# Weights and matmul operands moved to other byte positions in SBUF by padding

## The chip, the core and the metric

One core of a Trainium2 chip runs the program. The metric is the device time of one execution in microseconds. The kernel before took 2636.11 us as the median of three runs (2630.96 to 2636.66).

## What is computed

A stack of transformer blocks on 256 tokens of width 1024 in fp32. Two layers work on two streams, `x` and `ctx`: a gated feed-forward (1024 to 2816 and back), a token mixer (neighbourhood attention with a pooled branch, and attention to the context), and a second feed-forward; each is normed, modulated and added back. Then the stream `x` alone goes through a dilated attention mixer, a feed-forward, a chunkwise mLSTM mixer, and a last feed-forward and norm. Nearly all of the arithmetic is `h @ w` with a weight matrix that is read once:

```python
def swiglu(h, w_gate_up, w_down):
    gate, up = jnp.split(h @ w_gate_up, 2, axis=-1)
    return (jax.nn.silu(gate) * up) @ w_down
```

## The kernel before, in words

Activations lie transposed: 128 of the 1024 channels on the partitions, 8 such rows `k`, and the 256 tokens along the free dimension. A product keeps fp32 accuracy with three matmuls in the format fp32r: weight and operand are each split into a high and a low part, and `wh*xh`, `wh*xl` and `wl*xh` are added up in one PSUM bank. So each 128x128 block of a weight is loaded three times (`whi`, `whi`, `wlo`), and each load is followed by one matmul that streams 256 columns, or 258 where two columns carry the shift of the modulation.

The weights come as pieces of 1024 columns (4096 bytes in each partition). `Weights.fetch` (lines 80 to 85) has SP load a piece into one of three buffers `raw`; `Weights.cut` (lines 87 to 98) has ScalarE round it into `whi` and VectorE subtract that into `wlo`, each in a ring of six buffers. `wk` (lines 129 and 130) takes block k, 512 bytes wide, out of a piece. The pool `raw` and the pool `w` are opened in `build` (lines 1508 and 1509), right behind the constants.

The normed stream is `hh` and `hl`, one pair for each of the streams a and b (lines 1529 to 1533): 8 rows of `NP` = 272 floats, of which 258 are used. `gemm` (lines 270 to 280) streams row k of `hh`, `hl`, `hh` against block k of each of its weights, k from 0 to 7: this is the gate and up product (tile `gu`), the mixers' projections (`qkv`, `qk`, `ps_v`, `ps_o`). The way back is `blocks` (lines 587 to 602, matmuls on lines 598 to 600): it streams the rows of `s.ah` and `s.al`, 1024 bytes each, into `ps_dn` (feed-forward) or `ps_wo` (mixers). Where those tiles are allocated is in `ffn_two` (tiles `aha`, `ala`, `ahb`, `alb`), `ffn_one` (`ah`, `al`, one stream), `token_mix` (`oha`, `ola`, `ohb`, `olb`), `dilated_mix` and `mlstm_mix` (`oh`, `ol`). The order of the instructions on TensorE is the program's own (`manual_schedule`): a matmul waits only for its operands and its bank.

In a partition the tiles of the pools lie one behind the other in the order in which they are opened, each rounded up to 32 bytes. Counted in bytes of a partition, the tiles that TensorE reads start at:

| tile | before, start modulo 1024 | step from row to row |
|---|---|---|
| `whi`, `wlo`, every buffer | 96 | 512 (a block) |
| `hha`, `hla` | 480, 992 | 1088 |
| `hhb`, `hlb` | 512, 0 | 1088 |
| `aha`, `ala`, `ahb`, `alb`, `oha`, `ola`, `ohb`, `olb` | 544 | 1024 |
| `ah`, `al`; `oh`, `ol` of both single-stream mixers | 512 | 1024 |
| `pth`, `ptl` of the dilated mixer (streamed) | 768 | 1024 |
| `vh`, `vl` of the dilated mixer (loaded), groups 0 and 1 | 768 | 512 |

Of the kernel before, what the change touches and what calls it, by code (L numbers as in the profile page):

```python
# [9 lines left out]
F32 = mybir.dt.float32  # L10
F32R = mybir.dt.float32r
# [7 lines left out]
P = 128  # L19
T = 256  # L20
NS = 258
NP = 272
D = 1024
KD = D // P
FF = 2816
# [107 lines left out]
class Kernel:  # L133
# [9 lines left out]
    def plan(self):  # L143
# [27 lines left out]
        def mix(l):  # L171
# [5 lines left out]
            wout(("wo", l), A["w_out"][l])  # L177

        ffn_two(0, 0)
        mix(0)  # L180
        ffn_two(0, 1)
        ffn_two(1, 0)
        mix(1)
        ffn_one(("f", 1, 1), A["w_gu"][1, 1], A["w_down1"])
        for b in range(36):
            pair(("att",), A["attn_w_in"][b])
        wout(("awo",), A["attn_w_out"])
        ffn_one(("s", 0), A["ffn_w_in"][0], A["ffn_w_out"][0])
        p.append((("mg",), A["mlstm_gates"]))
        for b in range(12):  # L190
            pair(("ml",), A["mlstm_w_in"][b])
        wout(("mwo",), A["mlstm_w_out"])
        ffn_one(("s", 1), A["ffn_w_in"][1], A["ffn_w_out"][1])
        return p

# [431 lines left out]
    def ffn_two(self, l, i, first, nxts, start):  # L627

        nc = self.nc
        key = ("f", l, i)  # L630
        n = 0 if i == 0 else 2
        mods = self.mods[l, i]
        sa, sb = self.pair
        with ExitStack() as es:
            self.fp = pool = es.enter_context(self.tc.tile_pool(name="ffn", bufs=1))
            for s in self.pair:
                s.ah = pool.tile([P, HF, T], F32R, name="ah" + s.name)
                s.al = pool.tile([P, HF, T], F32R, name="al" + s.name)
                s.y = pool.tile([P, KD, T], F32, name="y" + s.name)

            def evac(s, ps, jj):
                self.defer(s.ch, lambda: self.gu_evac(s, ps, jj, NS))

            for h in range(2):
                for jj in range(HF):
                    j = h * HF + jj
                    if j < len(first):
                        w, ps = first[j]
                        evac(sa, ps, jj)
                        evac(sb, self.gu_mm(sb, w, NS, together=j == 0), jj)  # L650
                    else:
                        if j == len(first):
                            self.drain(sa.ch)
                            self.load_cond(pool)
                            self.mod_plan = deque(m for n in mods for m in mods[n])
                        w = self.gu_weights(key, j)
                        for s in self.pair:
                            evac(s, self.gu_mm(s, w, NS), jj)
                            self.drain(s.ch)
                    self.mod_chunks(mods.get(j, ()))  # L660
                w = Chunks(lambda: self.W.get(key + ("dn",)))
                for s, ds in self.lagged(self.pair, LAG if h else 0):
                    if s is sa:
                        for d in ds:
                            self.mod_chunks(mods.get(KF + h * KD + d, ()))
                    for d, ps in self.blocks(s, ds, lambda d, c: w(HF * d + c), HF, "ps_dn"):
                        y = s.y[:, d, :]
                        if h == 0:
                            nc.scalar.activation(out=y, in_=ps, func=AF.Copy)
                            continue  # L670
                        with self.tc.high_priority(offset=FIRST):
                            nc.vector.tensor_tensor(out=y, in0=ps, in1=y, op=ALU.add)
                            if d == 0:
                                s.acc = self.new_acc(s)
                            self.square_into(s.acc, y, d == 0)
                        if d == KD - 1:
                            self.post(s, self.g5(s, l, n), s.y, nxts[s.i], WAIT[s.i])
            return self.handover(start, sa, sb)
# [13 lines left out]
    def ffn_one(self, key, s, n, first, post, nxt, start):  # L692

        nc = self.nc
        with ExitStack() as es:
            self.fp = pool = es.enter_context(self.tc.tile_pool(name="ffn", bufs=1))
            s.ah = pool.tile([P, KF, T], F32R, name="ah")
            s.al = pool.tile([P, KF, T], F32R, name="al")
            y = pool.tile([P, KD, T], F32, name="y") if post else None
            for j in range(KF):  # L700
                if j < len(first):
                    ps = first[j][1]
                else:
                    if j == len(first):
                        self.drain(s.ch)
                    ps = self.gu_mm(s, self.gu_weights(key, j), n)
                self.defer(s.ch, lambda ps=ps, j=j: self.gu_evac(s, ps, j, n))
            acc = None
            w = Chunks(lambda: self.W.get(key + ("dn",)))
            for ds in ((0, 1), *((d,) for d in range(2, KD))):  # L710
                for d, ps in self.blocks(s, ds, lambda d, c: w(KF * d + c), KF, "ps_dn"):
                    if post:
                        self.keep(s, d, ps, y[:, d, :])
                    else:
                        acc = self.residual(s, d, ps, nxt, acc)
            if post:
                self.post(s, post, y, (nxt, None), WAIT[2])
            return self.handover(start, s)
# [508 lines left out]
    def mlstm_mix(self, s, first, nxt, start):  # L1227
        with ExitStack() as es:
            op = es.enter_context(self.tc.tile_pool(name="mlo", bufs=1))
            s.ah = op.tile([P, KD, T], F32R, name="oh")  # L1230
            s.al = op.tile([P, KD, T], F32R, name="ol")
            self.mp = es.enter_context(self.tc.tile_pool(name="ml", bufs=2))
            att, vch = self.mlstm_core(s, first)
            self.wout_one(("mwo",), s, nxt, att, 2)
            self.end(vch, att)
            return self.handover(start, s)
# [251 lines left out]
    def build(self):  # L1488
        tc, nc, A = self.tc, self.nc, self.A
# [14 lines left out]
        with ExitStack() as es:  # L1504
            ec = es.enter_context
            ec(tc.manual_schedule(engines={mybir.EngineType.PE}))
            self.const = const = ec(tc.tile_pool(name="const", bufs=1))
            rawp = ec(tc.tile_pool(name="raw", bufs=RAW))
            wp = ec(tc.tile_pool(name="w", bufs=RING))
            self.tmp = ec(tc.tile_pool(name="tmp", bufs=2))  # L1510
            self.psp = ec(tc.tile_pool(name="psp", bufs=8, space=PSUM))
            self.wch = self.chain()
            self.W = Weights(tc, rawp, wp, self.plan(), RING - 1, 3)
# [5 lines left out]
            self.ident = self.cst("ident")  # L1519
            self.modv = [const.tile([P, NMODC, 2], F32, name="modv%d" % l) for l in range(2)]  # L1520

            sa, sb = self.pair = [Stream(), Stream()]
            hp_a = ec(tc.tile_pool(name="sa", bufs=1))
            es_b = ExitStack()
            hp_b = es_b.enter_context(tc.tile_pool(name="sb", bufs=1))
            for i, (s, hp) in enumerate(((sa, hp_a), (sb, hp_b))):
                s.i, s.name = i, "ab"[i]
                s.ch = self.chain()
                s.x = hp.tile([P, KD, T], F32, name="x" + s.name)
                s.hh = hp.tile([P, KD, NP], F32R, name="hh" + s.name)  # L1530
                s.hl = hp.tile([P, KD, NP], F32R, name="hl" + s.name)
                s.r = hp.tile([P, NS], F32, name="r" + s.name)
                nc.vector.memset(s.r[:, T:NS], 1.0)

            nx = lambda l, n: [(self.gs1(s, l, n), (l, n)) for s in self.pair]
            fin = lambda name, o=0: (lambda c: self.par(name, o + c, 1))
# [187 lines left out]
```

## Time and profile before

| | |
|---|---|
| median of three runs | 2636.11 us |
| the profiled execution | 2636.68 us |
| its span, first to last instruction | 2634.9 us |
| mean granted TensorE clock | 0.97 of full speed |
| TensorE matmuls | 20335, busy 2527.3 us |
| weight loads | 20335, busy 2451.9 us |
| VectorE, ScalarE, GpSimd busy | 1857.8, 1171.5, 75.2 us |

Matmuls overlap in the profile (one is shown as some 0.28 us long), so what a matmul costs is read as the distance from one start to the next in the timeline, not from its length.

### The profile page before, as it was taken

To read this page: it belongs to the slowest core of one execution; us is meant where nothing else is said; L and a number is where in the kernel's file an instruction comes from. 1 tells how busy PE (TensorE), PEld (TensorE's weight loads), DVE (VectorE), ACT (ScalarE), POOL (GpSimd) and SP (SyncE) were. 2 spreads that over 40 slices of the span, in tenths; PEclk is the share of its full clock that TensorE was granted. 3 is DMA by queue.
4 is the path that set the end of the run, shared out by engine and by line. 5 is a ranking of instruction groups with operands and counts; after the bars stand their busy time and mean duration, and the time that the engine had idled before them with its cause. 6 is when DMAs were issued, how large, how long until landed. Compare 5 with 4: busy or idle time off the path is not lost. (4 is left out here: it accounts for less than half of the span.)

```text
span 2634.9 us, 49868 instructions
## 1 busy us (share of the span) xinstructions
PE 2527.3 (96%) x20335; PEld 2451.9 (93%) x20335; DVE 1857.8 (71%) x3734; ACT 1171.5 (44%) x2062; POOL 75.2 (3%) x131
## 2 busy tenths in 40 slices
PE   7999998999999999999999888998999999999998
PEld 5999997889999999999998778998999999978998
DVE  5998548676998546984547767757888676666764
ACT  4332324664432333332334555545655554565542
POOL 0000001210000000000000310000000000000000
PEclk9999998999999999999999988999999999988999
DMA  8666323622566321674222734554444365533653
GB/s 300 205 212 207 105 89 74 79 45 73 184 204 222 103 96 58 225 254 153 97 93 77 87 69 149 195 184 136 149 149 149 131 205 181 173 104 103 202 176 120
DMA packets 105254, 383.17 MB, mean 145 GB/s; under 512 B 13560, under 2 KB 13688, under 8 KB 103360
## 3 DMA queue, kind: packets, MB, share of 16 engines
q1 hardware_dynamic: 101984, 370.89, 42.2%
q0 software_dynamic: 3040, 9.09, 4.3%
q8 instruction: 159, 2.61, 0.4%
q14 instruction: 71, 0.58, 0.1%
HBM read 378.88 MB, written 1.05 MB: 144 GB/s over the span
## 5 line engine op out<-in xcount | busy, mean ns | idle before, releaser
L94 ACT ACTIVATE whi<-raw 128x1024 fp32r<-128x1024 f32 x559 | 588.3, 1054 | 566.3 <-PE gu L278 172.4
L96 DVE TENSOR_TENSOR wlo<-raw,whi 128x1024 fp32r<-128x1024 f32 x559 | 680.8, 1220 | 222.8 <-ACT whi L94 220.3
L279 PE MATMUL gu<-hha,wlo 128*128 128x258 f32 (+1 forms) x2112 | 602.4, 285 | 9.0 <-DVE wlo L96 9.0
L277 PE MATMUL gu<-hha,whi 128*128 128x258 f32 (+1 forms) x2112 | 601.8, 285 | 4.3 <-ACT hha L254 2.5
L278 PE MATMUL gu<-hla,whi 128*128 128x258 f32 (+1 forms) x2112 | 602.5, 285 | 1.0 <-DVE hla L255 1.0
L279 PEld LDWEIGHTS gu<-hha,wlo 128*128 128x128 f32 x2112 | 406.5, 192 | 10.8 <-DVE wlo L96 10.8
L277 PEld LDWEIGHTS gu<-hha,whi 128*128 128x128 f32 x2112 | 406.5, 192 | 5.4 <-ACT hha L254 3.1
L278 PEld LDWEIGHTS gu<-hla,whi 128*128 128x128 f32 x2112 | 405.4, 192 | 2.0 <-DVE hla L255 1.9
L278 PE MATMUL gu<-hlb,whi 128*128 128x258 f32 x1056 | 301.1, 285 | 1.3 <-DVE hlb L255 1.0
L277 PE MATMUL gu<-hhb,whi 128*128 128x258 f32 x1056 | 299.8, 284 | 1.1 <-ACT hhb L254 1.1
L279 PE MATMUL gu<-hhb,wlo 128*128 128x258 f32 x1056 | 295.9, 280 | 0.0
L278 PEld LDWEIGHTS gu<-hlb,whi 128*128 128x128 f32 x1056 | 200.6, 190 | 2.3 <-DVE hlb L255 2.3
L277 PEld LDWEIGHTS gu<-hhb,whi 128*128 128x128 f32 x1056 | 200.6, 190 | 1.5 <-ACT hhb L254 1.5
L279 PEld LDWEIGHTS gu<-hhb,wlo 128*128 128x128 f32 x1056 | 202.0, 191 | 0.0
L503 DVE SCALAR_TENSOR_TENSOR junk<-wm,cond 128x1024 bf16<-128x1024 f32 x128 | 156.3, 1221 | 41.9 <-DMA wm<-w_mod 41.0
L599 PE MATMUL ps_dn<-ala,whi 128*128 128x256 f32 x528 | 146.2, 277 | 2.2 <-DVE ala L252 2.2
L599 PE MATMUL ps_dn<-al,whi 128*128 128x256 f32 x528 | 148.2, 281 | 0.0
L598 PE MATMUL ps_dn<-ah,whi 128*128 128x256 f32 x528 | 148.2, 281 | 0.0
L600 PE MATMUL ps_dn<-ah,wlo 128*128 128x256 f32 x528 | 148.2, 281 | 0.0
L598 PE MATMUL ps_dn<-ahb,whi 128*128 128x256 f32 x528 | 147.7, 280 | 0.0
L599 PE MATMUL ps_dn<-alb,whi 128*128 128x256 f32 x528 | 147.1, 279 | 0.0
L600 PE MATMUL ps_dn<-ahb,wlo 128*128 128x256 f32 x528 | 147.1, 279 | 0.0
(413 smaller groups left out, 6024.4 us busy)
## 6 DMA issues: line engine op xcount, KB each, us to landing
raw<-w_gu SPq DMA_DIRECT2D x176, 512.0 KB, 3.8
wm<-w_mod SPq DMA_DIRECT2D x128, 512.0 KB, 4.2
raw<-w_down SPq DMA_DIRECT2D x88, 512.0 KB, 3.4
raw<-ffn_w_in SPq DMA_DIRECT2D x88, 512.0 KB, 3.6
raw<-attn_w_in SPq DMA_DIRECT2D x72, 512.0 KB, 3.4
raw<-ffn_w_out SPq DMA_DIRECT2D x44, 512.0 KB, 3.3
raw<-w_in SPq DMA_DIRECT2D x32, 512.0 KB, 3.3
raw<-mlstm_w_in SPq DMA_DIRECT2D x24, 512.0 KB, 3.5
```

The costliest lines, as they stand in the source:

```text
L94: nc.scalar.activation(out=hi[:, :n], in_=raw[:, :n], func=AF.Copy)
L96: nc.vector.tensor_tensor(out=lo[:, :n], in0=raw[:, :n], in1=hi[:, :n].bitcast(F32), op=ALU.subtract)
L277: nc.tensor.matmul(o, wh, xh, start=k == 0, stop=False)
L278: nc.tensor.matmul(o, wh, xl, start=False, stop=False)
L279: nc.tensor.matmul(o, wl, xh, start=False, stop=k == KD - 1)
L503: nc.vector.scalar_tensor_tensor(out=out, in0=w, scalar=1.0, in1=self.cond[:, i, :], op0=ALU.mult, op1=ALU.mult, accum_out=m[:, i:i + 1],)
L598: nc.tensor.matmul(o, wh, xh, start=i == 0, stop=False)
L599: nc.tensor.matmul(o, wh, xl, start=False, stop=False)
L600: nc.tensor.matmul(o, wl, xh, start=False, stop=i == n - 1)
```

## The change

It adds padding and reorders the allocation, and nothing else: no instruction is added or removed. The row of the streams `hh`, `hl` becomes 288 floats (1152 bytes) in stream a and 320 floats (1280 bytes) in stream b. The two tiles `r` move from the stream's pool into the pool of constants, followed by 864 bytes of padding; the pool `tmp` gets 640 bytes; `ffn_two` gets 512 bytes ahead of stream b's tiles, `ffn_one` 256 bytes ahead of `ah`, and `mlstm_mix` 64 bytes ahead of `oh`.

```diff
-NP = 272
+NP = 288, 320
...
             for s in self.pair:
+                if s is sb:
+                    pool.tile([P, 128], F32, name="padb")
                 s.ah = pool.tile([P, HF, T], F32R, name="ah" + s.name)
...
+            pool.tile([P, 64], F32, name="pado")
             s.ah = pool.tile([P, KF, T], F32R, name="ah")
...
+            op.tile([P, 16], F32, name="padm")
             s.ah = op.tile([P, KD, T], F32R, name="oh")
...
             self.const = const = ec(tc.tile_pool(name="const", bufs=1))
+            sa, sb = self.pair = [Stream(), Stream()]
+            for s, n in zip(self.pair, "ab"):
+                s.r = const.tile([P, NS], F32, name="r" + n)
+            const.tile([P, 216], F32, name="pad")
...
             self.tmp = ec(tc.tile_pool(name="tmp", bufs=2))
+            self.tmp.tile([P, 160], F32, name="padt", bufs=1)
...
                 s.ch = self.chain()
+                nc.vector.memset(s.r[:, T:NS], 1.0)
                 s.x = hp.tile([P, KD, T], F32, name="x" + s.name)
-                s.hh = hp.tile([P, KD, NP], F32R, name="hh" + s.name)
-                s.hl = hp.tile([P, KD, NP], F32R, name="hl" + s.name)
-                s.r = hp.tile([P, NS], F32, name="r" + s.name)
-                nc.vector.memset(s.r[:, T:NS], 1.0)
+                s.hh = hp.tile([P, KD, NP[i]], F32R, name="hh" + s.name)
+                s.hl = hp.tile([P, KD, NP[i]], F32R, name="hl" + s.name)
```

Added up in the same way, the starts modulo 1024 become: `whi`, `wlo` 0; `hha`, `hla` 0 with rows 1152 bytes apart; `hhb`, `hlb` 0 with rows 1280 bytes apart; `aha`, `ala` 0; `ahb`, `alb` 512; `oha`, `ola`, `ohb`, `olb` 0; `ah`, `al` 256; `oh`, `ol` 0 in the dilated mixer and 64 in the mLSTM mixer.

## Rows read from the trace of the kernel before

**Rows 1.** The page, part 1 (busy us, share, count) and granted clock in 40 slices.
```profile
PE 2527.3 (96%) x20335; PEld 2451.9 (93%) x20335; DVE 1857.8 (71%) x3734; ACT 1171.5 (44%) x2062; POOL 75.2 (3%) x131
...
PEclk9999998999999999999999988999999999988999
```
**Rows 2.** Waits of TensorE, longest in total (us, times, longest).
```profile
PE ps_bc L315 <- DVE rt L292: 23.4, 10, 6.1
```
**Rows 3.** TensorE by line and shape (xcount, busy us, mean ns).
```profile
L277 PE MATMUL gu<-hha,whi 128*128 128x258 f32 x1408 | 403.8, 287 | 4.3 <-ACT hha L254 2.5 <-ACT whi L94 1.1 <-DVE hhb L340 0.8
...
L277 PE MATMUL gu<-hhb,whi 128*128 128x258 f32 x1056 | 299.8, 284 | 1.1 <-ACT hhb L254 1.1
...
L599 PE MATMUL ps_dn<-al,whi 128*128 128x256 f32 x528 | 148.2, 281 | 0.0
...
L599 PE MATMUL ps_dn<-ala,whi 128*128 128x256 f32 x528 | 146.2, 277 | 2.2 <-DVE ala L252 2.2
...
L277 PE MATMUL qkv<-hhb,whi 128*128 128x258 f32 x192 | 64.2, 335 | 3.2 <-ACT hhb L254 2.9
...
L598 PE MATMUL ps_wo<-oh,whi 128*128 128x256 f32 x128 | 37.6, 294 | 0.0
...
L598 PE MATMUL ps_wo<-oha,whi 128*128 128x256 f32 x128 | 35.8, 279 | 0.0
...
L598 PE MATMUL ps_wo<-ohb,whi 128*128 128x256 f32 x64 | 18.0, 281 | 0.0
```
**Rows 4.** Timeline, two-stream down product: first and last of 20 matmuls (start, length us).
```profile
999.79 0.28 PE L599 MATMUL ps_dn<-ala,whi 128*128 128x256 f32 x1
...
1001.94 0.28 PE L600 MATMUL ps_dn<-aha,wlo 128*128 128x256 f32 x1
```
**Rows 5.** Timeline of the weight loads in the same stretch: one load.
```profile
999.90 0.19 PEld L598 LDWEIGHTS ps_dn<-aha,whi 128*128 128x128 f32 x1
```
**Rows 6.** Timeline, a later two-stream down product: first and last of 19.
```profile
1189.79 0.28 PE L598 MATMUL ps_dn<-ahb,whi 128*128 128x256 f32 x1
...
1191.91 0.28 PE L598 MATMUL ps_dn<-aha,whi 128*128 128x256 f32 x1
```
**Rows 7.** Timeline, first single-stream down product: first and last of 19.
```profile
1742.82 0.28 PE L599 MATMUL ps_dn<-al,whi 128*128 128x256 f32 x1
...
1744.98 0.28 PE L599 MATMUL ps_dn<-al,whi 128*128 128x256 f32 x1
```
**Rows 8.** Timeline, second single-stream down product: first and last of 20.
```profile
2261.87 0.28 PE L599 MATMUL ps_dn<-al,whi 128*128 128x256 f32 x1
...
2264.10 0.28 PE L600 MATMUL ps_dn<-ah,wlo 128*128 128x256 f32 x1
```
**Rows 9.** Timeline, gate and up over four banks: row 5 (11 matmuls), row 6 (10).
```profile
2102.53 0.28 PE L277 MATMUL gu<-hha,whi 128*128 128x256 f32 x1
...
2103.66 0.28 PE L278 MATMUL gu<-hla,whi 128*128 128x256 f32 x1
...
2104.47 0.28 PE L277 MATMUL gu<-hha,whi 128*128 128x256 f32 x1
...
2105.55 0.28 PE L277 MATMUL gu<-hha,whi 128*128 128x256 f32 x1
```
**Rows 10.** Timeline, last head of the dilated mixer: first and 13th weighted sum.
```profile
2074.86 0.28 PE L264 MATMUL ps_pv<-pth,vh 128*128 128x256 f32 x1
...
2076.30 0.28 PE L264 MATMUL ps_pv<-pth,vh 128*128 128x256 f32 x1
```
**Rows 11.** Timeline, gate and up of stream b: first and last of 48.
```profile
859.33 0.28 PE L277 MATMUL gu<-hhb,whi 128*128 128x258 f32 x1
...
864.95 0.28 PE L279 MATMUL gu<-hhb,wlo 128*128 128x258 f32 x1
```
**Rows 12.** Timeline, three projections of stream a: ten starts, nine in row 2.
```profile
415.89 0.28 PE L277 MATMUL qkv<-hha,whi 128*128 128x258 f32 x1
...
416.98 0.28 PE L277 MATMUL qkv<-hha,whi 128*128 128x258 f32 x1
```

More of the change, by code (lines that the diff above doesn't have):

```diff
@@ L1520, in build @@
             self.modv = [const.tile([P, NMODC, 2], F32, name="modv%d" % l) for l in range(2)]
-            sa, sb = self.pair = [Stream(), Stream()]
             hp_a = ec(tc.tile_pool(name="sa", bufs=1))
```

## The prediction

> **What bounds the kernel now.** I read the page first: TensorE is busy in 96% of the span and its clock, shown in 40 slices, stands at 9 tenths or more of full speed in all but five of them [rows 1], a mean of 0.97 of the 2.4 GHz level. The longest entry in TensorE's list of waits is 23.4 us in all, under 1% of the span [rows 2]. So the end is set by the stream of matmuls itself, and a change that adds no instruction can move it only through how far apart two matmuls start. That distance is not on the page. It is in the timeline: (last start − first start) divided by the matmuls between. Starts are given to 10 ns, so a distance over ten matmuls is good to about 1 ns.
>
> The reader should see there that matmuls of one shape, at the full clock, run at different steady distances. The two-stream down product starts one each (1001.94−999.79)/19 = 113.2 ns [rows 4]; the same line 190 us later (1191.91−1189.79)/18 = 117.8 ns [rows 6]; the single-stream one 120.0 ns [rows 7] and, in the next feed-forward, 117.4 ns [rows 8]. The next block of weights is loaded while a matmul streams: a load starts at 999.90, with the matmul of that time [rows 5]. Two readers are thus in SBUF at once, and the table of starts says where.
>
> I call **relation** the start of the streamed row minus the start of the weight block, modulo 256 bytes, and sort the distances by it (weights stand at 96 now):
> - 192 (544−96): 113.2 or 117.8 ns [rows 4, 6]; row 5 of a normed stream (480+5×1088, also 192): (2103.66−2102.53)/10 = 113.0 ns [rows 9].
> - 160 (512−96): 120.0 or 117.4 ns [rows 7, 8].
> - 0: row 6 of the same stream, 2 us after row 5, same weights, same line: (2105.55−2104.47)/9 = 120.0 ns [rows 9]. The last head of the dilated mixer, where both operands start at 768: (2076.30−2074.86)/12 = 120.0 ns [rows 10].
>
> Of the last two, one pair stands 96 bytes past a multiple of 256 and the other on one, and the distance is the same. So the trace says that alignment as such does nothing, the relation does, and 0 is its worst steady value. That is a reading from few places; the choice rests on it.
>
> **The change, part by part.** After it the weights start at 0, `aha`, `ala`, `oha` to `olb` at 0, `ahb`, `alb` at 512, `ah`, `al` at 256, the dilated `oh` at 0: relation 0 everywhere on the way back, except the mLSTM mixer's 64. Stream b's rows, 1280 bytes apart, all have relation 0; stream a's, 1152 apart, have 0 and 128 by turns. Counts are those of the lines [rows 3]; three lines (L277 to L279, or L598 to L600) carry the same count.
>
> 1. *Two-stream down products*: 6 lines of 528 = 3168 matmuls. I read five of the six halves at the distance of [rows 4] and one at that of [rows 6]. To 120.0: 2640×(120.0−113.2) + 528×(120.0−117.8) = 18.0+1.2 = **+19.1 us**.
> 2. *Single-stream down products*: 3×528 matmuls; the first feed-forward is at 120.0 already [rows 7], the others at 117.4 [rows 8]: 1056×2.6 = **+2.7 us**.
> 3. *Products behind the mixers* (`ps_wo`): (128+64)×3 = 576 of the two-stream layers from the 113.2 ns of relation 192 to 120.0: +3.9 us; 192 of the dilated mixer from the 117.4 of relation 160 to 120.0: +0.5 us; 192 of the mLSTM mixer to relation 64, which none of my rows shows: between 113.2 and 120.0 it is −0.8 to +0.5 us, taken as 0. Together **+4.4 us**.
> 4. *Stream b's normed rows*: (1056+192)×3 = 3744 matmuls of 258 columns. Today their relation changes with k through 160, 224, 32, 96, and they start (864.95−859.33)/47 = 119.6 ns apart [rows 11]. At relation 0 nine matmuls of that width on one row took (416.98−415.89)/9 = 121.1 ns [rows 12]. **+5.6 us**. From below: the least steady distance anywhere, 113.2, would make it −24 us.
> 5. *Stream a's normed rows*: 4992 matmuls of 258 columns (1408×3 and 256×3 in `qkv`) and 4416 of 256. Today the relation goes through 128, 192, 0, 64; after, through 0 and 128, two of the same four, again changing with every third matmul. I take **0**. At the ends: all at 113.2 gives 4992×(119.6−113.2) = 32 us and, for 256 columns, from 116.5, the middle of [rows 9], 4416×3.3 = 15 us, so −47 us; all at relation 0's distances gives 4992×1.5 + 4416×3.5 = +23 us.
> 6. *All else*: the padding moves `raw` and all tiles behind it, so loads, ScalarE and VectorE work on other addresses. VectorE is busy 71% and ScalarE 44% [rows 1], both under TensorE; their waits are the fraction of a per cent above, and no row shows a cost by address. 0; if ScalarE and VectorE grew slower, `wlo` would be late, and the loads of `raw` behind it. The two `memset` of `r` only stand earlier in the program.
>
> Sum: 19.1+2.7+4.4+5.6 = +31.8 us. The profiled execution took 2636.7 us (span 2634.9), 0.6 us above the median of the three, so I sum against it: **2668 us**, 1.2% slower. About 0.2% (5.3 us) is what a measurement of this kernel can tell from no change.
>
> A rule would make the sum 0. On weights and operand together, the Trainium skill (SBUF — State Buffer, section "Who interferes with whom") gives TensorE two independent read ports, one for the moving operand and one for the weight load, and says that "PE and ACT never wait on anyone". By it no address could matter here and the time would stay at 2636.7 us. The trace does not agree: 113.0 and 120.0 ns, 2 us apart, with nothing changed but the row [rows 9].
>
> **Rivals.**
> - *Faster: a constant start wins.* Today a normed row's start moves by 64 bytes (modulo 256) with every third matmul, so no steady distance is reached in the stages with the most matmuls. If rows that keep one relation settle as [rows 4] do, stream b gains 3744×(119.6−113.2) = 24 us; if stream a settles too, 47 us more (step 5); if the single-stream down products follow, 1584×(118.3−113.2) = 8 us. It decides in the gate and up products, and from the point where they gain more than the 26 us of steps 1 to 3. Alone for stream b, with the ways back left at 113.2: 2613 us; all of it: 2558 us. For it: the settled stretches are among the fastest of the trace. Against it: relation 0 settled at 120.0 in both places that show it, and at 121.1 with 258 columns.
> - *No difference: the distance is a state and not an address.* The same tiles run at 113.2 and at 117.8 [rows 4, 6], and those of relation 160 at 120.0 and 117.4 [rows 7, 8]; which one they fall into was settled by what ran before. If the padding only draws these lots anew, gains and losses cancel: 2637 us, within some 5 us. Against it: [rows 9], where row 5 and row 6 differ in the way that the relation says.
> - *Slower, but less*: the down products keep 117.8 in place of 120.0. Then step 1 is 2640×4.6 = 12 us and the whole about +22 us: 2659 us. It belongs to the forecast.
>
> The page on TensorE (the Trainium skill, TensorE: Matmul & The Clock Gate, "Back-to-back issue gap") puts the gap at N/2.4+2.5, an estimate of 109.2 ns for 256 columns; no steady stretch that I read went under 113.0 ns.
>
> **How the numbers follow.** The forecast, slower by 10 to 49 us, gets 0.53: its rows are direct for steps 1 to 3, thin for 4 and 5. The faster rival gets 0.34, more than its few rows would give it, because steps 4 and 5 hold most of the matmuls and I saw 258 columns at a constant relation for nine of them only. No difference gets 0.13. Faster by over 0.2% is the second case, 0.34; within 0.2% is 0.12 of the third; slower is the first and the rest, 0.54. The range's upper end is the forecast with three quarters of step 5's upper end, 2668+17 = 2685. Its lower end takes in stream b's rival and a third of stream a's: 2613−16 = 2597. What is left out is the greater part of stream a's gain and the last quarter above. The forecast's own range is 2647 to 2685.
>
> **What would show it.** Right: in the timeline after, two-stream down products start 120.0 ns apart in place of 113.2; single-stream ones 120.0 in both places; stream b's gate and up products near 121, stream a's near 119.6; the same clock, the same counts, no new entry in the list of waits. Wrong: any settled stretch at relation 0 under 117 ns; gate and up products at 114; a list of waits with `wlo` or `raw` in it, which would say that step 6 was the one that counts.

## The result, and the profile after

The changed kernel took 2665.28 us as the median of four runs (2663.12 to 2670.19), the kernel before 2636.39 us beside it (2630.96 to 2637.36): a ratio of 1.0124, 95% interval 1.0107 to 1.0141. It is slower by 1.2%; the forecast was 2668.

The page of the changed kernel, part 1 and the granted clock in 40 slices (its span is 2661.7 us, where that of before was 2634.9):

```profile
PE 2553.3 (96%) x20335; PEld 2476.9 (93%) x20335; DVE 1859.3 (70%) x3734; ACT 1172.8 (44%) x2062; POOL 74.1 (3%) x131
...
PEclk9999998999999999999999889999999999988999
```

Set beside [rows 1]: the counts are the same, VectorE and ScalarE are busy for as long as before, and TensorE alone is busy 26.0 us longer. That is nearly the whole difference of the two spans, 26.8 us. So the time did not go into a wait. The list of waits of TensorE says the same (waited for, total us, times, longest):

```profile
PE ps_bc L315 <- DVE rt L292: 26.7, 10, 8.6
PE gu L279 <- DVE wlo L96: 8.8, 9, 3.1
```

The first stood at 23.4 us [rows 2]. The second, the weight cut `wlo` for which step 6 watched, stood in the kernel before at

```profile
PE gu L279 <- DVE wlo L96: 9.0, 9, 3.2
```

The timeline of the changed kernel shows where the time is (start us, length us; first and last of an unbroken row of matmuls):

```profile
866.95 0.28 PE L277 MATMUL gu<-hha,whi 128*128 128x258 f32 x1
...
872.62 0.29 PE L279 MATMUL gu<-hha,wlo 128*128 128x258 f32 x1
872.75 0.28 PE L277 MATMUL gu<-hhb,whi 128*128 128x258 f32 x1
...
878.43 0.28 PE L279 MATMUL gu<-hhb,wlo 128*128 128x258 f32 x1
...
1009.83 0.29 PE L600 MATMUL ps_dn<-aha,wlo 128*128 128x256 f32 x1
...
1012.95 0.28 PE L599 MATMUL ps_dn<-alb,whi 128*128 128x256 f32 x1
...
1764.79 0.28 PE L600 MATMUL ps_dn<-ah,wlo 128*128 128x256 f32 x1
...
1767.31 0.28 PE L600 MATMUL ps_dn<-ah,wlo 128*128 128x256 f32 x1
```

The two-stream down product: (1012.95−1009.83)/26 = 120.0 ns, in place of the 113.2 of [rows 4]. The single-stream one: (1767.31−1764.79)/21 = 120.0. Gate and up: (872.62−866.95)/47 = 120.6 ns in stream a, (878.43−872.75)/47 = 120.9 in stream b, in place of 119.6 [rows 11]. Each shift is small; some 18,000 distances carry them.

The same reading for the whole trace, worked out from all starts in it: the distances from one matmul's start to the next at the full clock and under 135 ns, by product, with their means and what the difference is worth at the changed kernel's counts.

```
product (columns)             before: n, ns      after: n, ns    us
two-stream down (256)         3140  114.17      3157  119.97   +18.3
single-stream down (256)      1582  118.23      1582  119.99    +2.8
ps_wo, two streams (256)       563  114.24       556  119.83    +3.1
ps_wo, one stream (256)        354  117.43       358  118.85    +0.5
stream b's normed rows (258)  3537  119.64      3562  120.46    +2.9
stream a's normed rows (258)  4700  119.81      4752  120.82    +4.8
stream a's normed rows (256)  4249  118.07      4259  118.84    +3.3
all others                    1059   96.90      1077   97.16    +0.3
distances of 135 ns and more                                    +1.3
stretches at the lowered clock (511 distances before, 397 after)   -10.2
sum                                                            +27.1
```

The row above the sum is the 24.0 us less that the changed kernel's trace spends at the lowered clock, set against the 13.8 us that these matmuls took at the full clock instead. TensorE ran for less time at its lower level in this execution. First the kernel before, then the changed one (span, mean granted clock):

```profile
core 0: 2634.9 us, clock 0.970
core 0: 2661.7 us, clock 0.975
```

The kernel before shows a swing of that size by itself, so nothing here says that the change raised the clock: in 43 runs of it made beside the experiments, on three chips, its time goes from 2623.81 us (clock 0.977) to 2642.04 us (0.969), mean 2632.2 at 0.9735. The execution that the prediction was summed against was one at a low clock. At like clocks the change costs about 34 us (four runs of the changed kernel: mean 2666.0 at 0.974). The sum of the table without that row is 37.3 us, 3 us more.

### The profile page after: what moved, and what is told of

Read it like the earlier page. It is cut to its first block, busy times and chain, and to the rows that moved or that the text cites. A ratio compares the mean times of both kernels' runs of the same rounds, so it can differ in the third digit from the quotient of the medians.

```text
span 2661.7 us, 49867 instructions
## 1 busy us (share of the span) xinstructions
PE 2553.3 (96%) x20335; PEld 2476.9 (93%) x20335; DVE 1859.3 (70%) x3734; ACT 1172.8 (44%) x2062; POOL 74.1 (3%) x131
## 5 line engine op out<-in xcount | busy, mean ns | idle before, releaser
L598 PE MATMUL ps_dn<-aha,whi 128*128 128x256 f32 x528 | 149.5, 283 | 0.0
L600 PE MATMUL ps_dn<-aha,wlo 128*128 128x256 f32 x528 | 149.5, 283 | 0.0
```

Of the source, the lines that this page charges most:

```text
L598: nc.tensor.matmul(o, wh, xh, start=i == 0, stop=False)
L600: nc.tensor.matmul(o, wl, xh, start=False, stop=i == n - 1)
```

## Experiments

The first six are the changed kernel with one thing moved; the others move more, and say what. "Distance" in the expectations is what the prediction calls relation: streamed row minus weight block, modulo 256 bytes.

### 1. Everything moved by 96 bytes

```diff
-            const.tile([P, 216], F32, name="pad")
+            const.tile([P, 240], F32, name="pad")
```

> All buffers behind the first constants move up by 96 bytes, so nothing starts on a multiple of 1024 any more (weights at 96 mod 256), while every distance from a weight block to a streamed row is that of the changed kernel. Theory R (the distance mod 256 bytes between streamed row and weight block sets the spacing): nothing changes, 120.0 ns in both streams' down products, 2665 us within 5. Rival A (the weights' own place on a multiple of 256 or 1024 slows them): the down products go back to 113 to 118 ns, the time to about 2636 us. Rival S (the two spacings are a state that is drawn anew, not an address): 113 or 120 ns by chance, between 2633 and 2670 us.

Measured: 2664.02 us (2657.98 to 2667.95), ratio to before 1.0123 (1.0083 to 1.0164). Timeline of the two kinds of down product:

```profile
1009.80 0.28 PE L600 MATMUL ps_dn<-ahb,wlo 128*128 128x256 f32 x1
...
1012.91 0.28 PE L599 MATMUL ps_dn<-ala,whi 128*128 128x256 f32 x1
...
1763.82 0.28 PE L598 MATMUL ps_dn<-ah,whi 128*128 128x256 f32 x1
...
1766.94 0.28 PE L600 MATMUL ps_dn<-ah,wlo 128*128 128x256 f32 x1
```

They run (1012.91−1009.80)/26 = 119.6 ns and (1766.94−1763.82)/26 = 120.0 ns apart, and the mean of each product in the table above comes back to within 0.1 ns. Nothing lies on a multiple of 1024 any more, and nothing has changed. The multiples of 1024 do nothing by themselves.

### 2. The weights alone moved by 64 bytes

```diff
-            const.tile([P, 216], F32, name="pad")
+            const.tile([P, 232], F32, name="pad")
...
-            self.tmp.tile([P, 160], F32, name="padt", bufs=1)
+            self.tmp.tile([P, 144], F32, name="padt", bufs=1)
```

> The changed kernel with the weights alone moved up by 64 bytes (64 mod 256 and no longer on multiples of 1024); every streamed row stays where the changed kernel has it, so that all distances become 192 mod 256 (64 for every second normed row of stream a). Theory R: only the distance counts, so the down products and output projections run at 113.3 or 117.8 ns in place of 120.0, as when the rows were moved instead: some 5,650 matmuls by 2.2 to 6.6 ns, 12 to 37 us less than 2665, that is 2628 to 2653 us. Rival (the rows' own start decides, on 256-byte boundaries 120.0): no change, 2665 us.

(The buffers `raw`, which TensorE does not read, move with the weights.) Measured: 2626.20 us (2621.91 to 2633.33), ratio 0.9975 (0.9956 to 0.9994): 64 bytes undo the loss and a little more. Its timeline:

```profile
994.97 0.28 PE L599 MATMUL ps_dn<-alb,whi 128*128 128x256 f32 x1
...
998.48 0.28 PE L600 MATMUL ps_dn<-ahb,wlo 128*128 128x256 f32 x1
...
1739.83 0.28 PE L600 MATMUL ps_dn<-ah,wlo 128*128 128x256 f32 x1
...
1743.91 0.28 PE L600 MATMUL ps_dn<-ah,wlo 128*128 128x256 f32 x1
...
2407.09 0.28 PE L599 MATMUL ps_wo<-ol,whi 128*128 128x256 f32 x1
...
2409.49 0.28 PE L598 MATMUL ps_wo<-oh,whi 128*128 128x256 f32 x1
```

(998.48−994.97)/31 = 113.2 ns and (1743.91−1739.83)/36 = 113.3 ns, with every streamed row where the changed kernel has it. The last two lines are the mLSTM mixer's product. Its rows begin at 64, so that it goes from distance 64 to 0, which the expectation overlooked, and it alone among the ways back gets slower: (2409.49−2407.09)/20 = 120.0 ns, where its mean in the changed kernel was 117.8. The time lies 2 us below the range expected; stream a's 256-column rows gained too, from 118.84 to 117.13 ns, 7 us that the expectation left out. Together with the first run this settles what the prediction rested on two places for: neither the weights' address nor the row's decides alone, but their distance.

### 3. The ways back alone at distance 192

```diff
...
+            pool.tile([P, 48], F32, name="pada")
             for s in self.pair:
...
-            pool.tile([P, 64], F32, name="pado")
+            pool.tile([P, 48], F32, name="pado")
...
+            op.tile([P, 48], F32, name="padx")
...
+            op.tile([P, 48], F32, name="padd")
...
-            op.tile([P, 16], F32, name="padm")
+            op.tile([P, 48], F32, name="padm")
```

> Weights and normed rows stay as in the changed kernel; only the operands of the ways back (down products and output projections) are padded to a constant distance of 192 bytes mod 256 from the weights. Theory R: the 3168 two-stream and 1056 single-stream down products of 256 columns times three operands' parts run at 113.3 ns in place of 120.0 (or at 117.8, the other spacing that the kernel before showed at 192): 12672 of 20335 matmuls is an overcount, so by the counts of the trace, 4224 down products and some 640 projections by 6.6 ns, 32 us less, about 2633 us; with 117.8 ns 11 us less, about 2654 us. Rival A: the weights are still on multiples of 1024, so 120.0 ns stays and 2665 us. Rival S: no relation to the pads, 2665 us or a chance value.

Measured: 2641.55 us (2637.52 to 2644.91), ratio 1.0034 (1.0019 to 1.0049); 22.5 us less than the first run, on the same chip. That is between the two forecasts of the theory (also with all 5,700 matmuls of the ways back counted, of which the expectation left out some 800), and the timeline shows why:

```profile
1176.78 0.28 PE L598 MATMUL ps_dn<-aha,whi 128*128 128x256 f32 x1
...
1179.96 0.28 PE L598 MATMUL ps_dn<-aha,whi 128*128 128x256 f32 x1
...
1189.93 0.28 PE L598 MATMUL ps_dn<-ahb,whi 128*128 128x256 f32 x1
1190.35 0.39 PE L599 MATMUL ps_dn<-alb,whi 128*128 128x256 f32 x1
...
1191.83 0.28 PE L599 MATMUL ps_dn<-ala,whi 128*128 128x256 f32 x1
...
1194.32 0.28 PE L600 MATMUL ps_dn<-aha,wlo 128*128 128x256 f32 x1
...
1749.73 0.28 PE L600 MATMUL ps_dn<-ah,wlo 128*128 128x256 f32 x1
...
1752.32 0.28 PE L598 MATMUL ps_dn<-ah,whi 128*128 128x256 f32 x1
...
2249.79 0.28 PE L600 MATMUL ps_dn<-ah,wlo 128*128 128x256 f32 x1
...
2252.39 0.28 PE L599 MATMUL ps_dn<-al,whi 128*128 128x256 f32 x1
```

In one stage, on the same tiles, the matmuls run (1179.96−1176.78)/27 = 117.8 ns apart; behind the one at 1189.93 the next is late by some 0.3 us; shortly after they run (1194.32−1191.83)/22 = 113.2 ns apart, and go on so for the next 38 us. The first single-stream down product keeps (1752.32−1749.73)/22 = 117.7 for all its 62 us, the second (2252.39−2249.79)/23 = 113.0 for its 60. Distance 192 has two steady spacings. In the down products of the kernel before, of this run and of the next, every changeover between them follows a distance of 0.35 us or more.

### 4. The same kernel a second time

> The kernel with only the ways back at 192, unchanged, executed and profiled a second time. In its first profile the three single-stream down products ran 117.8, 113.4 and 113.4 ns apart, and the first two-stream stage 117.8 to its end. If the program's own order and addresses settle which of the two spacings is taken, the same values come back stage by stage; if it is drawn in each execution, one or more of the nine half stages shows the other of the two values. Time 2637 to 2645 us.

Measured: 2637.87 us, one run. The same two places in its timeline:

```profile
1191.83 0.28 PE L598 MATMUL ps_dn<-ahb,whi 128*128 128x256 f32 x1
...
1194.31 0.28 PE L598 MATMUL ps_dn<-aha,whi 128*128 128x256 f32 x1
...
1749.83 0.28 PE L599 MATMUL ps_dn<-al,whi 128*128 128x256 f32 x1
...
1752.32 0.28 PE L600 MATMUL ps_dn<-ah,wlo 128*128 128x256 f32 x1
```

They have changed over: (1194.31−1191.83)/21 = 118.1 ns where it was 113.2, and (1752.32−1749.83)/22 = 113.2 where it was 117.7. The other down products kept their values. So at 192 the distance does not settle the spacing by itself: two executions of one program can end in different ones in the same stage. What decides between them, and how late a matmul must be for it, was not tried.

### 5. All distances in one run

Each down product gets a pad of its own (the operand's distance is the pad's size, plus what lies ahead of it):

```diff
+SCAN = {(0, 0): (32, 32), (0, 1): (64, 32), (1, 0): (128, 96), ("f", 1, 1): 96, ("s", 0): 160, ("s", 1): 192}
...
-                if s is sb:
-                    pool.tile([P, 128], F32, name="padb")
+                r = SCAN[l, i][s.i]
+                if r:
+                    pool.tile([P, r // 4], F32, name="pad" + s.name)
...
-            pool.tile([P, 64], F32, name="pado")
+            pool.tile([P, SCAN[key] // 4], F32, name="pado")
```

> The changed kernel, with each down product's operand at a distance of its own from the weights: 32 and 64 bytes mod 256 (streams a and b of the first two-stream stage), 64 and 96, 128 and 224, then 96, 160 and 192 in the three single-stream stages. Theory R: the spacing follows the distance wherever it comes: 64 about 117.8 ns, 128 about 118.7, 160 either 117.3 or 120.0, 192 113.3 or 117.8; for 32, 96 and 224 the kernel before had no steady rows, so anything from 113 to 122. Equal distances in two stages (64; 96) give equal spacings. Rival A: 120.0 ns everywhere. Rival S: one value per stage with no tie to the distance, 64 and 64 or 96 and 96 unlike. Time 2640 to 2668 us.

Measured: 2656.77 us, one run. Timeline, in order of time: distance 64 (stream b) twice, 96 (stream b of a later stage), 96 (single stream), 192 (single stream):

```profile
186.37 0.28 PE L599 MATMUL ps_dn<-ahb,whi 128*128 128x256 f32 x1
...
188.98 0.28 PE L601 MATMUL ps_dn<-ahb,wlo 128*128 128x256 f32 x1
...
217.16 0.28 PE L599 MATMUL ps_dn<-ahb,whi 128*128 128x256 f32 x1
...
219.76 0.28 PE L600 MATMUL ps_dn<-alb,whi 128*128 128x256 f32 x1
...
1008.84 0.28 PE L599 MATMUL ps_dn<-ahb,whi 128*128 128x256 f32 x1
...
1011.48 0.29 PE L600 MATMUL ps_dn<-alb,whi 128*128 128x256 f32 x1
...
1769.83 0.29 PE L599 MATMUL ps_dn<-ah,whi 128*128 128x256 f32 x1
...
1772.95 0.28 PE L601 MATMUL ps_dn<-ah,wlo 128*128 128x256 f32 x1
...
2599.82 0.28 PE L599 MATMUL ps_dn<-ah,whi 128*128 128x256 f32 x1
...
2603.00 0.28 PE L600 MATMUL ps_dn<-al,whi 128*128 128x256 f32 x1
```

Distance 64: (188.98−186.37)/23 = 113.5 ns, and 30 us later (219.76−217.16)/22 = 118.2. Distance 96 in two stages with other tiles and other row starts: (1011.48−1008.84)/22 = 120.0 and (1772.95−1769.83)/26 = 120.0. Distance 192: (2603.00−2599.82)/28 = 113.6. The means over the whole stages are 117.3 at 32, 118.6 at 128, 117.3 at 160 and 118.3 at 224. The 117.3 at 32 is a mixture: in the first stage the blocks of 33 matmuls of stream a run at 116.7 or at 120.0 ns, those of stream b (64) at 113.3 or 117.8, and they change over where one stream's block follows the other's, with no late matmul. Distance 160 has more than one value too: 120.0 and 117.4 in the kernel before [rows 7, 8], 118.7 in two and 117.3 in the third single-stream down product of the run with 160 and 224 (experiment 7). Rival A, 120.0 ns everywhere, is out; rival S holds only as a choice between a few values at one distance.

### 6. The normed rows alone back at 1088 bytes

```diff
-NP = 288, 320
+NP = 272, 272
```

> The changed kernel with the normed rows of both streams back at 1088 bytes, so that their distance from the weights steps through 0, 64, 128, 192 mod 256 as the row advances; weights and ways back stay at distance 0. Theory R: down products and output projections stay at 120.0 ns; the 258-column matmuls fall from 120.4 to 121.0 ns to about 119.6, the mean of before's two streams, 11,000 of them by about 1.2 ns: 13 us less, 2652 us. Rival (the normed rows' part is nothing, as the prediction had it for stream a): 2662 us or more. Rival (the normed rows carry the whole change): 2637 us.

Measured: 2657.56 us (2654.01 to 2660.42), ratio 1.0103 (1.0083 to 1.0122), 5 us above the 2652 expected; the expectation counted 11,000 matmuls of 258 columns, and there are 4992+3744 = 8736. The interval overlaps that of the change, so the time alone does not size this part; the spacings do. Gate and up of stream a:

```profile
866.49 0.28 PE L277 MATMUL gu<-hha,whi 128*128 128x258 f32 x1
...
872.11 0.28 PE L279 MATMUL gu<-hha,wlo 128*128 128x258 f32 x1
```

(872.11−866.49)/47 = 119.6 ns, where the changed kernel has 120.6. Over the whole trace, down products and `ps_wo` stay within 0.1 ns of the table's right-hand column; stream a's 258-column rows go from 120.82 back to 119.87, its 256-column rows from 118.84 to 118.14, stream b's from 120.46 to 119.87. Worked out as in the table, that is 4.5+3.0+2.1 = 9.6 us. So both streams' normed rows pay, not b's alone.

### 7. Is there a good constant distance for 258 columns?

Three runs. In the first every operand has distance 192 (both streams' rows 1280 bytes apart, one pad of 64 bytes ahead of `hha`, the other pads left out); the other two set stream a's and stream b's rows apart from each other by pads ahead of `hha` and `hhb`.

```diff
-NP = 288, 320
+NP = 320, 320
...
-            const.tile([P, 216], F32, name="pad")
+            const.tile([P, 24], F32, name="pad")
...
-            self.tmp.tile([P, 160], F32, name="padt", bufs=1)
...
+                if s is sa:
+                    hp.tile([P, 16], F32, name="padh")
```

> Distance 192 mod 256 for every operand that streams past weights: the ways back as in the run before, and the normed rows of both streams too (rows of 1280 bytes for both). Theory R: besides the 32 us of the ways back, the 11232 normed-row matmuls of 258 columns and 4419 of 256 columns drop from about 120.5 ns by something between nothing and 6.5 ns: the time between 2633 and about 2540 us, less what the throttle takes back. Rival A: weights on multiples of 1024, 2665 us. Rival that the two extra columns decide for normed rows: ways back gain alone, about 2633 us.

The pads of the second run, against those of the first, are 160 bytes ahead of `hha` and 32 ahead of `hhb`; those of the third 32 and 64. The ways back move with them: the two-stream down products to 64 and 224, the single-stream ones to 32 and 160.

```diff
+PADH = 40, 8
...
-                if s is sa:
-                    hp.tile([P, 16], F32, name="padh")
+                hp.tile([P, PADH[i]], F32, name="padh" + s.name)
```

> As the run with distance 192 everywhere, but stream a's normed rows at a constant 32 and stream b's (and both streams' down products) at a constant 64 mod 256. If 258-column matmuls have a good distance as 256-column ones have 192, one of 32, 64, 160, 224 (this run and the next) shows 115 ns or less, against 120.0 to 121.2 at 0, 128 and 192; if the two extra columns spoil any constant distance, all four lie within 119 to 122. Two-stream down products near 117.5 (64 in the scan: 117.0 to 118.0).

```diff
+PADH = 8, 16
...
-                if s is sa:
-                    hp.tile([P, 16], F32, name="padh")
+                hp.tile([P, PADH[i]], F32, name="padh" + s.name)
```

> The same with stream a's normed rows at 160 and stream b's, with the two-stream down products, at 224. The same two forecasts: 115 ns or less at one of them, or 119 to 122 at both. Two-stream down products near 118.3 (224 in the scan).

Measured: 2626.23 us (2621.83 to 2634.47, ratio 0.9982, 0.9964 to 1.0001) with 192 everywhere; 2650.31 and 2646.30 us, one run each. Timeline of the run with 32 and 64, stream b at 64, then stream a at 32:

```profile
871.57 0.28 PE L278 MATMUL gu<-hhb,whi 128*128 128x258 f32 x1
...
877.19 0.28 PE L279 MATMUL gu<-hlb,whi 128*128 128x258 f32 x1
877.44 0.28 PE L278 MATMUL gu<-hha,whi 128*128 128x258 f32 x1
...
882.84 0.28 PE L278 MATMUL gu<-hha,whi 128*128 128x258 f32 x1
```

and of the run with 160 and 224, stream b at 224:

```profile
866.63 0.28 PE L279 MATMUL gu<-hlb,whi 128*128 128x258 f32 x1
...
872.03 0.28 PE L279 MATMUL gu<-hlb,whi 128*128 128x258 f32 x1
```

(877.19−871.57)/46 = 122.2 ns at 64, (882.84−877.44)/45 = 120.0 at 32, (872.03−866.63)/45 = 120.0 at 224. Whole-trace means: 32 120.0, 64 121.3, 160 120.0, 192 120.9, 224 120.1, and 0 120.5 from the changed kernel's stream b. No constant distance tried takes 258 columns under 120.0 ns, while stream a's 256-column rows at 192 fall from 118.84 to 115.80. Of the 192-everywhere run's 38 us against the first run, the normed rows' share is those 256-column rows, 12.9 us, and nothing of the 258-column ones (8736 of them; the expectation's 11232 is a miscount).

### 8. Steps of 32 and 96 bytes

Against the run with 192 everywhere:

```diff
-NP = 320, 320
+NP = 264, 280
+PADH = 16, 8
...
-                if s is sa:
-                    hp.tile([P, 16], F32, name="padh")
+                hp.tile([P, PADH[i]], F32, name="padh" + s.name)
```

> Distance 192 (single stream) and 224 (two streams) for the ways back; the normed rows of stream a step by 32 bytes (1056 each), those of stream b by 96 (1120 each), through all eight distances. If stepping as such lowers the 258-column mean from 120.5 to 119.5 or so, as steps of 64 did, both streams lie within 119 to 120; if the step of 64 was a lucky one, 120 to 121. Time 2630 to 2650 us.

Measured: 2636.96 us, one run. Stream a, stepping by 32, has a mean of 119.7 ns for 258 columns, stream b, stepping by 96, 120.6. The one is like a step of 64 (119.6 to 119.9), the other like a constant distance. That stepping as such helps is not shown.

### 9. The best parts together

As the run with 192 everywhere, with stream b's rows at 1088 bytes and the distances 160, 224, 32, 96 of the kernel before.

```diff
-NP = 320, 320
+NP = 320, 272
+PADH = 16, 56
...
-                if s is sa:
-                    hp.tile([P, 16], F32, name="padh")
+                hp.tile([P, PADH[i]], F32, name="padh" + s.name)
...
+                if s is sb:
+                    hp.tile([P, 8], F32, name="padq")
```

(The pad `padq` behind `hlb` brings the tiles after it to 192.)

> The run with distance 192 everywhere, with stream b's normed rows alone back at 1088 bytes and at the four distances of the kernel before (160, 224, 32, 96 mod 256). Theory R: down products stay at 113.3 to 114, stream b's 258-column rows go from 120.8 back to 119.5 as the mean of before's (118.4 twice, 121.9 once), 3750 by 1.3 ns: 5 us less than that run, 2621 us, 0.4 per cent under the kernel before. Rival (rows' steps do nothing): 2626 us as that run.

Measured: 2617.45 us (2611.64 to 2631.89), ratio 0.9948 (0.9928 to 0.9969). Gate and up of stream b:

```profile
862.35 0.28 PE L278 MATMUL gu<-hhb,whi 128*128 128x258 f32 x1
...
867.84 0.29 PE L279 MATMUL gu<-hlb,whi 128*128 128x258 f32 x1
```

(867.84−862.35)/46 = 119.3 ns; its whole-trace mean is 119.61 against 120.86 in the run with 192 everywhere, 4 us. The time is 4 us under the 2621 expected. This version beats both kernels: half a per cent under the one before. By the spacings that is from the 256-column products of stream a (118.07 to 115.71 ns, 10.0 us) and the single-stream down products (118.23 to 114.82, 5.4 us).

## Why the prediction was right

The sign, the size and the mechanism held. Two steps were taken at a wrong price, and that the time came out within 3 us of the forecast is in part luck, as the sum below shows.

- *What bounds the kernel.* Right: the counts, the other engines' busy times and the list of waits are as before, and TensorE's busy time has grown by the difference.
- *Relation decides, alignment does nothing, 0 is the worst steady value.* The first two are shown by runs 1 and 2. The last needs a correction: 96 is as slow as 0 (120.0 ns, run 5), and with 258 columns 64 is slower than 0 (run 7).
- *Step 1*, +19.1 us: +18.3. *Step 2*, +2.7: +2.8. *Step 3*, +4.4: +3.6 (3.1 and 0.5). The mLSTM mixer's relation 64, taken as nothing, runs at 117.8 ns, within the two bounds it was given.
- *Step 4*, +5.6: +2.9. The 121.1 ns of [rows 12] came from nine matmuls on one row; 3562 such distances have a mean of 120.46.
- *Step 5*, 0: +8.1 (4.8 and 3.3). This is the term that was mis-sized. "Two of the same four, again changing with every third matmul" was not enough to keep the mean: rows that alternate between 0 and 128 run at 120.82 ns, rows that step through all four at 119.81, and run 6 brings that back by the rows alone. The value lies between 0 and the step's upper end, +23, in the lower half.
- *Step 6*, 0: 0.3 us, plus 1.3 of longer distances that no run ties to the padding.
- *The sum*: 31.8 predicted. By the table 36.0 for all products, 1.3 of longer distances, and 10.2 us that the higher clock of that execution gave back. Steps 4 and 5 were off by 5.4 us together, and the clock hid this, which was luck: a sum against one execution also carries that execution's clock, 0.970 here, at which the 43 runs of before lie near their slow end.
- *The rule of two independent read ports* (the Trainium skill, SBUF — State Buffer, "Who interferes with whom"), taken to mean that no address matters, is contradicted here a second time: with the weights moved by 64 bytes and every streamed row left in place, the same rows go from 120.0 to 113.2 ns. Where weight load and streamed row meet, no run shows. The 109.2 ns that the prediction quotes (the Trainium skill, TensorE: Matmul & The Clock Gate, "Back-to-back issue gap") is what that section gives for the gap of an isolated matmul; no settled stretch of 256 columns that was read here went under 113.0 ns.

*The rivals.* "Faster: a constant start wins" fell where it had placed itself, in the gate and up products: 258 columns settle at 120.0 ns or more at every constant relation tried. It holds for 256 columns at relation 192, which the change did not choose. "No difference: a state and not an address" holds in part: at one relation there can be two spacings or more (runs 3 to 5). But at relation 0 only one was seen: every down product of the changed kernel, of run 1 and of run 6 has a mean of 119.9 to 120.0 ns. So moving to 0 cost something instead of drawing anew. "Slower, but less" fell with 120.0.

## What to carry to other kernels

When a kernel is bound by back-to-back matmuls, read the distance between starts in the timeline, stage by stage, and compare it with where the streamed row and the weight block begin. Here a pad of 64 bytes on one of the two was worth 39 us in 2665, and rounding both to a large power of two put them at a distance where 256 columns showed 120.0 ns and nothing faster. A sum made against one profiled execution should say at what granted clock that execution ran.

## What was not expected of the hardware

- One program, one address, two speeds: 113.3 or 117.8 ns at relation 192, kept for up to 62 us, in one stage the one in one execution and the other in the next. Relations 64, 32 and 160 show more than one value too.
- Two columns more undo the gain of a good distance: with 192 everywhere, stream a's normed rows have a mean of 115.8 ns with 256 columns and of 120.9 with 258.
- At the lowered clock the distance shows no effect: the median spacing there, of the distances from 180 to 260 ns, is 213 ns for `ps_wo` of two streams at relation 0 (11 of them, changed kernel), for the ways back at 160 and 192 (21 and 20, kernel before), and for all 256-column products at 192 (94, the run with 192 everywhere). With 258 columns it is 214 ns in all three.
- The kernel before swings by 18 us among 43 runs, the slower the lower its granted clock (0.969 to 0.979), more than half of what the change costs.
